# A mixer layer's output projection: residual and first y blocks loaded ahead, last row pair reordered

## The chip, the cores and the metric

One core of a Trainium2 chip runs the whole kernel. The metric is the device time of one execution in microseconds (us); before the change it is 945.74 us, the median of 3 runs (945.64 to 947.35). Engines are named as the profile names them: PE (TensorE; PEld its weight loads), DVE (VectorE), ACT (ScalarE), POOL (GpSimd) and SP (SyncE, which issues the DMAs here).

## The reference

One layer over 2048 tokens of width 1024, in float32. Branches A, B and C each make part of y; the change concerns the last line.

```python
h = jnp.einsum('bsd,de->bse', x, w_in)
a_u, a_v, a_g, b_val, b_glu, b_g, c_q, c_f, c_i, c_g = jnp.split(h, offsets, axis=-1)
y_a = _sgu_mixer(a_u, a_v, sgu_ln_g, sgu_ln_b, sgu_w, sgu_b) * jax.nn.silu(a_g)
y_b = _conv_module(b_val, b_glu, conv_w, conv_b, conv_ln_g, conv_ln_b) * jax.nn.silu(b_g)
y_c = _hgrn2_mixer(c_q, c_f, c_i, lb, hgrn_norm_g) * jax.nn.silu(c_g)
y = jnp.concatenate([y_a, y_b, y_c], axis=-1)
y = jnp.einsum('bse,ed->bsd', y, w_out)
return _layernorm(DEEPNORM_ALPHA * x + y, post_ln_g, post_ln_b)
```

## The kernel before, in words

The sequence is worked in two halves of two groups of 512 tokens. Each half runs branch B, then values, branch C and branch A in an order of its own (first half: B, A, values, C; second half: B, values, C, A), so that branch A of the second half stands right before the output projection. Every float32 matmul is made of three (`three`, L198): operands are split into a high and a low part (`split`, L144: a cast on ACT, a subtraction on DVE), and high x high, low x high and high x low are accumulated in one PSUM bank. Every branch stores its y, transposed, to `y_dr` in DRAM through SP (`y_store`, L229; the store at L230).

Branch A (`sgu`, L730) projects u and the gate for two feature tiles (ft) of two groups (gi); each ends with a mix matmul, `mx` (L632) and `ay` (L636) on DVE, and the store of ay. After a group, `free_c` (L782) is called: after group 0 it closes branch C's memory and loads blocks 0 to 2 of the transformed output weights (`wo_load`, L720, two DMAs of 1 MB a block, from `wo_dr`), and blocks 3 and 4 into the memory of that group's x; after group 1 blocks 5 and 6 into the memory of the last group's x.

The output projection takes 16 row blocks of 128 tokens as 8 pairs. A pair is a 2 x 2 block product in Strassen's manner (Winograd's form): seven products of 12 matmuls each (`product`, L842) of y blocks a11, a12, s2, s3, s1, a22, s4 with weight blocks wo[0], [1], [2], [3], [4], [6], [5]. `y_blocks` (L804) loads four raw pieces (ry) from y_dr, makes the sums (ysa, ysb; L833 to L837) and splits them into four tiles, a (a11, a12), s (s2, s3), t (s1, s4) and b (a22). The trace names the operands by these: `wh_y_a`, `wh_y_s`, `wh_y_t`, `wh_y_b`. Four of the products accumulate on one bank z (`poz`): a11, then s2, s1 and s4 on top of it, and between them DVE reads z out into the residual (`plus`, L884: alpha times x plus z); a12 goes into `poa`, s3 and a22 into `pod`, both added by `join` (L887). So a product onto z waits until the read-out ahead of it is done, and that read-out waits for the residual `xr`, which is loaded from x into one of four buffers (L879). `normed` (L849) then takes the layer norm of each row block: statistics on ACT (L859 to L862), for the very last row block on DVE (L854, L855); the reciprocal root on POOL (`rstd_of`, L223: an add and a power); two passes on DVE (L864, L867) and the store.

The order on each engine is not that of the program text: a scheduler orders the instructions at build time by a model of the chip's times, taking what is ready in the order of the text, and puts waits where data or memory require them. What stands late in the text can thus be executed early, if its memory is free. The order is fixed when the kernel runs; each engine and each DMA queue works through its own in order. A pool opened with `reuse_waits="tile"` waits for the release of each old tile that it covers, not of the whole pool.

Of the kernel before, what the change touches and what calls it, by code (L numbers as in the profile page):

```python
# [11 lines left out]
F32 = mybir.dt.float32  # L12
# [8 lines left out]
P = 128  # L21
# [62 lines left out]
def _body(tc, nc, d, ctx):  # L84
# [528 lines left out]
    def sgu_unit(g, gi, x, pl, vhat, w):  # L613
        if True:
            for ft in range(2):
# [15 lines left out]
                mx = pl.tile([P, 4, P], F32, tag="mx", bufs=2, name=f"mx{nm}")  # L631
# [98 lines left out]
    def sgu(hf, xs, pl, after):  # L730
# [3 lines left out]
        for gi in range(GPH):  # L734
            sgu_unit(hf * GPH + gi, gi, xs[gi], pl, vhat, w)
            after(gi)

    for hf in range(NHALF):
# [8 lines left out]
        if hf == 0:  # L747
            lower_bounds()
            sgu_setup()
            with ExitStack() as esw:  # L750
                wo_start(pool("wos", stack=esw, reuse_waits="tile"))
                with ExitStack() as esa:
                    pl = pool(f"a{hf}", stack=esa, reuse_waits="tile")
                    sgu(hf, xs, pl, lambda gi: None)
# [27 lines left out]
    def free_c(gi):  # L782
# [11 lines left out]
    with ExitStack() as esa:  # L794
        pl = pool("a1", stack=esa, side="right", reuse_waits="tile")
        sgu(NHALF - 1, xs, pl, free_c)


    NP = S // (2 * P)
    ot = pool("ot", stack=es, side="right", reuse_waits="tile")  # L800
    gb = ot.tile([P, 2, DM], F32, name="gb")
    nc.sync.dma_start(gb, d["post"])

    def y_blocks(p):  # L804
# [10 lines left out]
        out = {}  # L815
# [16 lines left out]
        pair("a", (a11, a12), ("a11", "a12"))  # L832
        nc.vector.tensor_add(s1, a21, a22)  # L833
        nc.vector.tensor_sub(s2, s1, a11)
        nc.vector.tensor_sub(s3, a11, a21)
        pair("s", (sa,), ("s2", "s3"))
        nc.vector.tensor_sub(s4, a12, s2)  # L837
        pair("t", (sb,), ("s1", "s4"))
        pair("b", (a22,), ("a22",))
        return out  # L840

    def product(out, y, blk, first):  # L842
        w = wo[blk].rearrange("p h (k n) -> p h k n", n=512)
        for kt in range(4):
            three(out, y[0][:, kt, :], y[1][:, kt, :], w[:, 0, kt, :], w[:, 1, kt, :],
                  first and kt == 0, kt == 3, skip_group_check=not first)
            tick(0.64)

    def normed(t, r, fine):  # L849
        mv = smp.tile([P, 2], F32, tag="omv", bufs=4, name=f"omv{t}")  # L850
        if fine:
            st = smp.tile([P, 2, 6], F32, name="ost")
            for n in range(2):
                nc.vector.bn_stats(st[:, n, :], r[:, n * 512 : (n + 1) * 512])  # L854
            nc.vector.bn_aggr(mv, st)  # L855
            rs = rstd_of(smp, mv[:, 1:2], 1, "ors")
        else:
# [101 lines left out]
```

## Time and profile before

| | before |
|---|---|
| median of 3 runs | 945.74 us (945.64 to 947.35) |
| the profiled execution: its time | 945.64 us |
| its span, first to last instruction | 943.9 us |
| PE busy | 912.6 us (97%) |
| PEld busy | 755.2 us (80%) |
| DVE busy | 710.6 us (75%) |
| ACT busy | 396.3 us (42%) |
| POOL busy | 81.7 us (9%) |
| mean granted TensorE clock | 0.989 |

Busy time is that of the span; matmuls overlap, so PE's busy share says only that matmuls follow one another. Times of the trace are counted from the span's start. The output projection is the stretch from 766.7 us to the end. The granted clock is a share of full speed: 1.0 is 2.4 GHz, 0.5 is 1.2 GHz. The shares of the whole span average over stages with different limits, so the rows below are all of single stretches.

### The profile page before, as it was taken

How to read it: one execution, taken by the hardware profiler on the slowest of the kernel's cores; microseconds unless marked ns; L12 is line 12 of the kernel's file. 1: busy time of each engine (PE TensorE's matmuls, PEld its weight loads, DVE VectorE, ACT ScalarE, POOL GpSimd, SP SyncE). 2: the span in 40 equal slices, each digit the busy share in tenths (PEclk: the TensorE clock that was granted, in tenths of full speed). 3: DMA queues.
4: the chain of work that ended last, by engine and by line, in shares of the span. 5: the costliest groups of instructions: out<-in, count | busy, mean ns of one | idle time of the engine just before them, and what ended most of it. 6: DMA issues, size and time to landing. Idle time of an engine off the chain costs nothing.

```text
span 943.9 us, 15786 instructions
## 1 busy us (share of the span) xinstructions
PE 912.6 (97%) x6045; PEld 755.2 (80%) x6045; DVE 710.6 (75%) x1605; ACT 396.3 (42%) x795; POOL 81.7 (9%) x129
## 2 busy tenths in 40 slices
PE   8999999999999999999999999999999996999994
PEld 6889888987777777788998777777798885888883
DVE  6998899736787669897997867778765235888885
ACT  6644363234354446542223435354544330634551
POOL 0001101000010000010000000000021000221121
PEclk9999999999999999999999999999999997999998
DMA  8756463111011104411111201111112987456422
GB/s 268 272 180 230 168 244 113 67 45 46 24 49 64 45 24 157 134 58 44 56 46 45 77 16 56 38 43 57 58 44 69 308 314 268 134 174 199 140 90 90
DMA packets 60812, 107.48 MB, mean 114 GB/s; under 512 B 5312, under 2 KB 21952, under 8 KB 60608
## 3 DMA queue, kind: packets, MB, share of 16 engines
q1 hardware_dynamic: 60736, 106.48, 33.0%
q8 instruction: 47, 0.77, 0.3%
q14 instruction: 29, 0.24, 0.1%
HBM read 75.00 MB, written 31.46 MB: 113 GB/s over the span
## 4 chain that ended last, share of the span: by engine, by line
PE 70%; DVE 16%; ACT 4%; DMA 3%; issue 3%; POOL 3%; SPq 0%; DVEq 0%; POOLq 0%; ACTq 0%
DVE acc L283 4%; PE poz L199 3%; PE pm_ci L200 3%; PE pm_ci L199 3%; PE pm_ci L201 3%; PE poz L200 3%; PE poz L201 3%; PE pm_q L199 3%; PE pm_q L201 3%; PE pm_q L200 3%; PE pm_f L199 2%; PE pm_f L200 2%; PE pm_f L201 2%; PE pm_cg L199 2%; PE pm_cg L201 2%
## 5 line engine op out<-in xcount | busy, mean ns | idle before, releaser
L283 DVE SCALAR_TENSOR_TENSOR acc<-bh,vec,acc 128x512 f32<-128x512 f32 x240 | 172.5, 746 | 2.2
L146 DVE TENSOR_TENSOR wl<-rw,wh 128x512 fp32r<-128x512 f32 x84 | 56.7, 686 | 29.2 <-ACT wh L145 29.2
L145 ACT CAST wh<-rw 128x512 fp32r<-128x512 f32 x84 | 50.1, 619 | 31.1 <-PE pm_f L200 11.1
L199 PE MATMUL pm_ci<-wh_ci,xhix 128*128 128x256 f32 x192 | 54.5, 284 | 0.0
L201 PE MATMUL pm_ci<-wh_ci,xlox 128*128 128x256 f32 x192 | 54.3, 283 | 0.0
L200 PE MATMUL pm_ci<-wl_ci,xhix 128*128 128x256 f32 x192 | 54.3, 283 | 0.0
L550 ACT ACTIVATE jk<-po 128x128 f32<-128x128 f32 x64 | 17.7, 277 | 60.7 <-PE po L545 59.8
L199 PE MATMUL pm_f<-xhix,wh 128*128 128x512 f32 x96 | 41.1, 429 | 0.0
L199 PE MATMUL pm_q<-xhix,wh 128*128 128x512 f32 x96 | 41.0, 427 | 0.0
L347 ACT COPY vh<-pm_ci 128x256 f32<-128x256 f32 x32 | 11.9, 373 | 65.7 <-PE pm_ci L201 65.6
L200 PE MATMUL pm_q<-xlox,wh 128*128 128x512 f32 x96 | 39.0, 407 | 0.0
L199 PE MATMUL pm_cg<-xhix,wh 128*128 128x512 f32 x96 | 39.0, 406 | 0.0
L201 PE MATMUL pm_q<-xhix,wl 128*128 128x512 f32 x96 | 37.8, 394 | 0.0
L201 PE MATMUL pm_f<-xhix,wl 128*128 128x512 f32 x96 | 37.8, 393 | 0.0
L200 PE MATMUL pm_f<-xlox,wh 128*128 128x512 f32 x96 | 37.6, 392 | 0.0
L201 PE MATMUL pm_cg<-xhix,wl 128*128 128x512 f32 x96 | 37.6, 391 | 0.0
L200 PE MATMUL pm_cg<-xlox,wh 128*128 128x512 f32 x96 | 37.5, 390 | 0.0
L199 PEld LDWEIGHTS pm_ci<-wh_ci,xhix 128*128 128x128 f32 x192 | 36.9, 192 | 0.0
L200 PEld LDWEIGHTS pm_ci<-wl_ci,xhix 128*128 128x128 f32 x192 | 36.9, 192 | 0.0
L201 PEld LDWEIGHTS pm_ci<-wh_ci,xlox 128*128 128x128 f32 x192 | 36.8, 192 | 0.0
L225 POOL TENSOR_SCALAR crs<-ss 128x4 f32<-128x4 f32 x16 | 3.6, 226 | 373.8 <-ACT jk L550 373.8
L884 DVE SCALAR_TENSOR_TENSOR xr<-xr,poz 128x512 f32<-128x512 f32 x32 | 21.7, 682 | 17.3 <-DMA xr<-x 13.2
(330 smaller groups left out, 2803.2 us busy)
## 6 DMA issues: line engine op xcount, KB each, us to landing
rw<-wf SPq DMA_DIRECT2D x84, 256.0 KB, 3.0
wob<-wo_dr SPq DMA_DIRECT2D x14, 1024.0 KB, 11.4
ry<-y_dr SPq DMA_DIRECT2D x32, 256.0 KB, 3.2
xr<-x SPq DMA_DIRECT2D x16, 512.0 KB, 4.4
out<-xr SPq DMA_DIRECT2D x15, 512.0 KB, 2.7
wo_dr<-wsh SPq DMA_DIRECT2D x28, 256.0 KB, 3.5
wo_dr<-wsl SPq DMA_DIRECT2D x28, 256.0 KB, 2.5
rx<-xT SPq DMA_DIRECT2D x24, 256.0 KB, 3.3
```

Of the source, the lines that this page charges most:

```text
L145: nc.scalar.copy(hi, src)
L146: nc.vector.tensor_sub(lo, src, hi.bitcast(F32))
L199: nc.tensor.matmul(out, wh, xh, start=first, stop=False, **kw)
L200: nc.tensor.matmul(out, wh, xl, start=False, stop=False, **kw)
L201: nc.tensor.matmul(out, wl, xh, start=False, stop=last, **kw)
L225: nc.gpsimd.tensor_scalar(r, mv_var, scale, EPS, ALU.mult, ALU.add)
L283: nc.vector.scalar_tensor_tensor(a, h[:, k : k + G], vcol(cw + k), a, ALU.mult, ALU.add)
L347: nc.scalar.copy(vh[:, gi * 4 + tt, vp * 256 : (vp + 1) * 256], pt[:, :256])
L550: nc.scalar.activation(jk, po[:, c * P : (c + 1) * P], AF.Square, accum_out=ss[:, c : c + 1])
L884: nc.vector.scalar_tensor_tensor(r[:, ns], r[:, ns], ALPHA, t, ALU.mult, ALU.add)
```

## The change

The residual `xr` gets a pool of its own, opened before branch A of the second half, and the loads for pairs 0 and 1 are issued there; later pairs are loaded two pairs ahead. `mx` and `ay` of branch A get one buffer instead of two. `y_blocks` becomes a generator, `y_steps`: its first two steps for pair 0 stand after ft 0 of group 1 in branch A, the rest after branch A; for later pairs the steps stand between the products of the pair before. The last pair gets an order of its own (a11, a12, s2, s4, s1, s3, a22): s4 goes to a bank of its own (z2), and a22 to another (d2), in two halves of 256 columns, each read out by itself. Both row blocks of the last pair take their statistics on DVE, piece by piece, and their reciprocal root as an add on DVE and a power on POOL. The diff, cut to its core:

```diff
-                mx = pl.tile([P, 4, P], F32, tag="mx", bufs=2, name=f"mx{nm}")
+                mx = pl.tile([P, 4, P], F32, tag="mx", bufs=1, name=f"mx{nm}")
...
-                y = pl.tile([P, G], F32, tag="ay", bufs=2, name=f"ay{nm}")
+                y = pl.tile([P, G], F32, tag="ay", bufs=1, name=f"ay{nm}")
...
+                after(gi, ft)
...
-    def free_c(gi):
+    def free_c(gi, ft):
+        if ft == 0:
+            if gi == 1:
+                first_y.append(y_steps(0))
+                for _ in range(2):
+                    next(first_y[0])
+            return
...
+    n0, n1 = slice(0, 512), slice(512, 1024)
+    ys, xr, first_y = {}, {}, []
+    xrp = pool("xr", stack=es, side="right", reuse_waits="tile")
+
+    def load_xr(p):
+        xr[p] = []
+        for k in range(2):
+            t = 2 * p + k
+            r = xrp.tile([P, DM], F32, tag="xr", bufs=4, name=f"xr{t}")
+            nc.sync.dma_start(r, d["x"][t * P : (t + 1) * P, :])
+            xr[p].append(r)
+
+    stiles = pool("stiles", stack=es, side="right")
+
+    def y_steps(p):
...
         pair("a", (a11, a12), ("a11", "a12"))
+        yield
         nc.vector.tensor_add(s1, a21, a22)
         nc.vector.tensor_sub(s2, s1, a11)
         nc.vector.tensor_sub(s3, a11, a21)
         pair("s", (sa,), ("s2", "s3"))
+        yield
         nc.vector.tensor_sub(s4, a12, s2)
         pair("t", (sb,), ("s1", "s4"))
+        yield
         pair("b", (a22,), ("a22",))
-        return out
-
-    def product(out, y, blk, first):
+
+    load_xr(0)
+    load_xr(1)
+    with ExitStack() as esa:
+        pl = pool("a1", stack=esa, side="right", reuse_waits="tile")
+        sgu(NHALF - 1, xs, pl, free_c)
+
+    for _ in first_y[0]:
+        pass
+
+
+    ot = pool("ot", stack=es, side="right", reuse_waits="tile")
+    gb = ot.tile([P, 2, DM], F32, name="gb")
+    nc.sync.dma_start(gb, d["post"])
+
+    def product(out, y, blk, first, cols=slice(0, 512)):
...
+    def store(t, r, rs, mv, parts):
         nc.vector.scalar_tensor_tensor(r, r, mv[:, 0:1], gb[:, 0, :], ALU.subtract, ALU.mult)
-        for n in range(2 if fine else 1):
-            ns = slice(n * 512, (n + 1) * 512) if fine else slice(0, DM)
+        for ns in parts:
             nc.vector.scalar_tensor_tensor(r[:, ns], r[:, ns], rs, gb[:, 1, ns], ALU.mult, ALU.add)
             nc.sync.dma_start(d["out"][t * P : (t + 1) * P, ns], r[:, ns])
 
...
+    def stats(t, r, parts):
+        st = smp.tile([P, len(parts), 6], F32, name=f"ost{t}")
+
+        def take(k):
+            nc.vector.bn_stats(st[:, k, :], r[:, parts[k]])
+
+        def done():
+            mv = smp.tile([P, 2], F32, tag="omv", bufs=4, name=f"omv{t}")
+            nc.vector.bn_aggr(mv, st)
+            rs = smp.tile([P, 1], F32, tag="orl", bufs=2, name=f"orl{t}")
+            nc.vector.tensor_scalar(rs, mv[:, 1:2], EPS, None, ALU.add)
+            nc.gpsimd.tensor_tensor(rs, rs, nhalf[:, :1], ALU.pow)
+            return rs, mv
+
+        return take, done
+
...
+        y = ys.pop(p)
+        r1, r2 = xr.pop(p)
+        ahead = y_steps(p + 1)
         z = bank("mm", 3, f"poz{p}")
         a = bank(("o", "st")[p % 2], 1, f"poa{p}")
         dd = bank("sc", 2, f"pod{p}")
-        product(z, y["a11"], 0, True)
-        plus(r1, n0, z)
-        product(a, y["a12"], 1, True)
-        product(z, y["s2"], 2, False)
-        plus(r2, n0, z)
-        join(r1, n0, a)
-        product(dd, y["s3"], 3, True)
-        product(z, y["s1"], 4, False)
-        plus(r2, n1, z)
-        join(r2, n1, dd)
-        product(dd, y["a22"], 6, False)
-        join(r2, n0, dd)
-        normed(2 * p + 1, r2, False)
-        product(z, y["s4"], 5, False)
-        plus(r1, n1, z)
-        normed(2 * p, r1, p == NP - 1)
+        if p < NP - 1:
+            product(z, y["a11"], 0, True)
+            plus(r1, n0, z)
+            product(a, y["a12"], 1, True)
+            next(ahead)
+            product(z, y["s2"], 2, False)
+            plus(r2, n0, z)
+            join(r1, n0, a)
+            product(dd, y["s3"], 3, True)
+            next(ahead)
+            product(z, y["s1"], 4, False)
+            plus(r2, n1, z)
+            join(r2, n1, dd)
+            product(dd, y["a22"], 6, False)
+            join(r2, n0, dd)
+            normed(2 * p + 1, r2)
+            product(z, y["s4"], 5, False)
+            for _ in ahead:
+                pass
+            plus(r1, n1, z)
+            normed(2 * p, r1)
+            if p + 2 < NP:
+                load_xr(p + 2)
+        else:
+            halves = (slice(0, 256), slice(256, 512))
+            take1, done1 = stats(2 * p, r1, (n0, n1))
+            take2, done2 = stats(2 * p + 1, r2, (n1,) + halves)
+            z2 = bank("mm", 3, f"poy{p}")
+            d2 = bank("sc", 2, f"poe{p}")
+            product(z, y["a11"], 0, True)
+            plus(r1, n0, z)
+            product(a, y["a12"], 1, True)
+            join(r1, n0, a)
+            take1(0)
+            product(z, y["s2"], 2, False)
+            plus(r2, n0, z)
+            product(z2, y["s4"], 5, True)
+            plus(r1, n1, z2)
+            product(z, y["s1"], 4, False)
+            join(r1, n1, z)
+            take1(1)
+            rs1, mv1 = done1()
+            plus(r2, n1, z)
+            product(dd, y["s3"], 3, True)
+            join(r2, n1, dd)
+            take2(0)
+            join(r2, n0, dd)
+            store(2 * p, r1, rs1, mv1, [slice(0, DM)])
+            for k, ns in enumerate(halves):
+                product(d2, y["a22"], 6, True, ns)
+                join(r2, ns, d2[:, ns])
+                take2(k + 1)
+            rs2, mv2 = done2()
+            store(2 * p + 1, r2, rs2, mv2, (n0, n1))
```

## Rows read from the trace of the kernel before

**Rows 1.** Stretches, projection's matmuls: bounds and length, PE and PEld busy (count), clock, DMA, GB/s.
```profile
766.60:780.60 14.00, 13.89 (x60) 11.19 (x60) 1.00 0.90 282
780.60:788.10 7.50, 0.00 (x0) 0.00 (x0) 0.66 1.03 417
788.10:793.40 5.30, 5.29 (x13) 4.18 (x14) 0.51 1.01 341
793.40:925.80 132.40, 132.13 (x577) 107.24 (x575) 1.00 0.43 144
```
**Rows 2.** Timeline of PE: start, duration, instruction, idle time before it and its releaser.
```profile
780.21 0.39 PE L201 MATMUL poa<-wob,wl_y_a 128*128 128x512 f32 x1
788.11 0.79 PE L199 MATMUL poz<-wob,wh_y_s 128*128 128x512 f32 x1 [7.51 <-DVE xr L884]
...
925.69 0.39 PE L201 MATMUL poz<-wob,wl_y_t 128*128 128x512 f32 x1
926.86 0.50 PE L199 MATMUL poz<-wob,wh_y_t 128*128 128x512 f32 x1 [0.78 <-DVE xr L884]
```
**Rows 3.** Chain that ended last, in order of time: start, length, what.
```profile
772.45 0.87 SPq L802
773.42 13.92 DMA xr<-x
```
**Rows 4.** Timeline of SP's DMA issues: start, length of merged issues, their count.
```profile
757.87 0.33 SPq L230 DMA_DIRECT2D y_dr<-ay  x1
765.78 0.52 SPq L724 DMA_DIRECT2D wob<-wo_dr  x1
769.57 0.33 SPq L230 DMA_DIRECT2D y_dr<-ay  x1
769.95 1.87 SPq L724 DMA_DIRECT2D wob<-wo_dr  x3
```
**Rows 5.** Timeline of DVE and POOL after the last matmul.
```profile
932.63 0.69 DVE L884 SCALAR_TENSOR_TENSOR xr<-xr,poz 128x512 f32<-128x512 f32 x1 [1.13 <-PE poz L201]
...
934.36 2.48 DVE L864 SCALAR_TENSOR_TENSOR xr<-xr,omv,gb 128x1024 f32<-128x1024 f32 x2
...
939.29 1.41 DVE L867 SCALAR_TENSOR_TENSOR xr<-xr,ors,gb 128x512 f32<-128x512 f32 x2 [0.72 <-POOL ors L226]
...
935.78 1.47 POOL L226 TENSOR_TENSOR ors<-ors,nhalf 128x1 f32<-128x1 f32 x1
...
938.70 0.55 POOL L226 TENSOR_TENSOR ors<-ors,nhalf 128x1 f32<-128x1 f32 x1
```
**Rows 6.** Timeline of ACT and DVE in branch A.
```profile
765.56 0.62 ACT L145 CAST wh_y_b<-ry 128x512 fp32r<-128x512 f32 x1 [2.48 <-PE pm_ag L200]
...
713.58 1.28 DVE L146 TENSOR_TENSOR wl<-rw,wh 128x512 fp32r<-128x512 f32 x2
```
**Rows 7.** Stretches: PE, PEld, DVE, ACT, POOL busy (count), clock, DMA share, GB/s.
```profile
671.00:684.00 13.00, 12.97 (x112) 10.49 (x112) 9.89 (x29) 6.50 (x21) 1.32 (x2) 1.00 0.17 62
...
828.00:847.00 19.00, 19.00 (x84) 15.45 (x83) 16.11 (x21) 8.53 (x15) 3.73 (x4) 1.00 0.49 166
```
**Rows 8.** Issues at 771.2 (wob) and 757.9 us (ay): size, us to landing.
```profile
wob<-wo_dr SPq DMA_DIRECT2D x1, 1024.0 KB, 12.4
...
y_dr<-ay SPq DMA_DIRECT2D x1, 256.0 KB, 11.1
```
**Rows 9.** DVE groups, 828 to 847 us: count | busy us, mean ns | idle before.
```profile
L146 DVE TENSOR_TENSOR wl_y_s<-ysa,wh_y_s 128x1024 fp32r<-128x1024 f32 x1 | 1.2, 1226 | 0.0
...
L834 DVE TENSOR_TENSOR ysa<-ysb,ry 128x512 f32<-128x512 f32 x1 | 0.7, 684 | 0.0
```
**Rows 10.** Timeline of PE and DVE in branch A: pieces of 256 columns.
```profile
690.02 0.28 PE L201 MATMUL pm_av<-wh_av,xlox 128*128 128x256 f32 x1
690.14 0.28 PE L199 MATMUL pm_av<-wh_av,xhix 128*128 128x256 f32 x1
...
714.86 0.43 DVE L607 BATCH_NORM_STATS2 ast<-vg 128x6 f32<-128x256 f32 x1
```

More of the change, by code (lines that the diff above doesn't have):

```diff
@@ L611, in sgu_values, with sgu_unit @@
         return vhat
-    def sgu_unit(g, gi, x, pl, vhat, w):
+    def sgu_unit(g, gi, x, pl, vhat, w, after):
         if True:
@@ L734, in sgu @@
         for gi in range(GPH):
-            sgu_unit(hf * GPH + gi, gi, xs[gi], pl, vhat, w)
-            after(gi)
+            sgu_unit(hf * GPH + gi, gi, xs[gi], pl, vhat, w, after)
     for hf in range(NHALF):
@@ L814, in y_blocks @@
         a11, a12, a21, a22 = raw
-        out = {}
+        out = ys[p] = {}
         def pair(nm, srcs, names):
@@ L843, in product @@
+    gb = ot.tile([P, 2, DM], F32, name="gb")
+    nc.sync.dma_start(gb, d["post"])
+    def product(out, y, blk, first, cols=slice(0, 512)):
         w = wo[blk].rearrange("p h (k n) -> p h k n", n=512)
         for kt in range(4):
-            three(out, y[0][:, kt, :], y[1][:, kt, :], w[:, 0, kt, :], w[:, 1, kt, :],
-                  first and kt == 0, kt == 3, skip_group_check=not first)
+            three(out[:, cols], y[0][:, kt, :], y[1][:, kt, :], w[:, 0, kt, cols],
+                  w[:, 1, kt, cols], first and kt == 0, kt == 3, skip_group_check=not first)
@@ L864, in normed @@
         nc.vector.scalar_tensor_tensor(r, r, mv[:, 0:1], gb[:, 0, :], ALU.subtract, ALU.mult)
[L865 to L866 removed]
+        for ns in parts:
             nc.vector.scalar_tensor_tensor(r[:, ns], r[:, ns], rs, gb[:, 1, ns], ALU.mult, ALU.add)
             nc.sync.dma_start(d["out"][t * P : (t + 1) * P, ns], r[:, ns])
+    def normed(t, r):
+        mv = smp.tile([P, 2], F32, tag="omv", bufs=4, name=f"omv{t}")
+        jk = ot.tile([P, DM], F32, tag="ojk", name=f"ojk{t}")
+        nc.scalar.activation(jk, r, AF.Identity, scale=1.0 / DM, accum_out=mv[:, 0:1])
+        nm = smp.tile([P, 1], F32, tag="onm", bufs=4, name=f"onm{t}")
+        nc.scalar.activation(nm, mv[:, 0:1], AF.Copy, scale=-1.0)
+        nc.scalar.activation(jk, r, AF.Square, bias=nm, accum_out=mv[:, 1:2])
+        store(t, r, rstd_of(smp, mv[:, 1:2], 1, "ors", 1.0 / DM), mv, [slice(0, DM)])
@@ L870, in _body, with plus, join @@
     smp = pool("smp", stack=es, side="right")
-    stiles = pool("stiles", stack=es, side="right")
-    n0, n1 = slice(0, 512), slice(512, 1024)
+    def plus(r, ns, t):
+        nc.vector.scalar_tensor_tensor(r[:, ns], r[:, ns], ALPHA, t, ALU.mult, ALU.add)
+    def join(r, ns, t):
+        nc.vector.tensor_add(r[:, ns], r[:, ns], t)
     for p in range(NP):
-        y = y_blocks(p)
-        xr = []
-        for k in range(2):
-            t = 2 * p + k
-            r = ot.tile([P, DM], F32, tag="xr", bufs=4, name=f"xr{t}")
-            nc.sync.dma_start(r, d["x"][t * P : (t + 1) * P, :])
-            xr.append(r)
-        r1, r2 = xr
-        def plus(r, ns, t):
-            nc.vector.scalar_tensor_tensor(r[:, ns], r[:, ns], ALPHA, t, ALU.mult, ALU.add)
-        def join(r, ns, t):
-            nc.vector.tensor_add(r[:, ns], r[:, ns], t)
+        y = ys.pop(p)
+        r1, r2 = xr.pop(p)
+        ahead = y_steps(p + 1)
```

25 lines of the change are left out of this document (2 added, 23 removed).

## The prediction, made before the change was run

> **What bounds the kernel now.** I read the stretches of the output projection first, then the matmuls around their gap, then the chain that ended last, the DMA issues, and last the tail. [rows 1]: the projection is bound by TensorE at the higher clock: 577 matmuls in 132.4 us, a pitch of 0.23 us. Three stretches are not. After five products (60 matmuls) no matmul runs for 7.5 us while the DMA share is 1.03, and then 13 matmuls take 5.3 us at a granted clock of 0.51 (the 1.2 GHz level). [rows 2]: the gap runs from 780.21 to 788.11 and its releaser is the first addition of the residual (L884), which reads xr. The matmul that waits, the s2 product of pair 0, accumulates on bank z, so z must be read out before it. [rows 3]: the chain of work goes from the issue of gb into one transfer of xr, 13.92 us from issue to landing. [rows 3, 4]: xr was issued at 773.42 behind three issues of wob and one of gb; the queue was full, not idle, as the DMA share of 1.03 in [rows 1] says. The third loss is in the last pair, [rows 2]: 0.78 us idle at 926.86, again a read-out of z. Last, TensorE ends at 932.63 where the final read-out begins, and the span ends at 943.9: a tail of 11.27 us [rows 5].
>
> Branch A, 714 to 766 us, is no target: the y blocks of pair 0 were already made there. The last of them, the cast for a22, runs at 765.56, before the projection's first matmul at 766.7 [rows 1, 6]. The scheduler had hoisted them although they stand behind branch A in the program. So of "prepared during branch A" only the residual is new.
>
> **The change, part by part.** All terms are against the profiled execution: 943.9 us of span and 945.64 of time, so 1.74 outside the span; that execution is 0.1 under the median of 945.74.
>
> *Residual loaded before branch A.* Four issues of 512 KB move past branch A's weight loads, its y stores and all fourteen wob issues on SP. Where they now stand the DMA share is 0.17 [rows 7], so 2 MB fit at the 417 GB/s of [rows 1] in 5 us. Behind them on SP stand weight loads whose buffers are split only from 713.58 [rows 6], some 30 us later; that cover hides them. What goes: the gap, 7.90 minus one pitch 0.23 = 7.67 us, and the slow stretch, 5.3 minus 13 x 0.23 = 2.3 us, since without idle time there is nothing after which the clock fell. Sum **-10.0**.
>
> *What is late next.* Without the wait on xr the products of pair 0 can follow one another: 12 x 0.23 = 2.73 us each, from 766.7. Their weights are the seven wob blocks. Block 6 is the last: its second half was issued at the end of the three merged issues (771.2) and took 12.4 us, landing at 783.6 [rows 4, 8]. Nothing in the change makes it earlier: its buffer is x of group 3, which branch A's last projection reads; block 5, held up in the same way, was first issued at 765.78 [rows 4]. With a11, a12, s2, s3, s1, s4 first, a22 wants it at 766.7 + 6 x 2.73 = 783.1: **+0.5 us**. In program order a22 comes before s4 and wants it at 780.4: +3.2 us, and perhaps the slow clock again (+2.3). Which it is depends on the scheduler's order, which the trace of before doesn't show; I take the first, because it did fill TensorE with products of pair 1 (five products before the gap, two of them of pair 1) rather than wait in program order. Ends for this term: 0 and +5.5.
>
> *mx and ay with one buffer.* mx is written and read on VectorE in order: nothing. ay now waits for the store of the ay before. The store issued at 757.87 took 11.1 us (769.0) [rows 4, 8], and the last ay was written 0.7 us before its store at 769.57, so from 768.85: a wait of 0.15 us. Behind it on VectorE stands the first read-out of z, which has a product (2.73 us) to spare; behind its store on SP stand three wob issues, so block 6 lands up to 0.15 later. Inside the 0.5 above.
>
> *y steps of the next pair between the products.* The same instructions as before in another program order; a pair takes VectorE 16.11 of 19 us, in which TensorE does the 84 matmuls of a pair without a gap [rows 7]. Before, they were hoisted likewise. I take 0; the bound above is the rival below.
>
> *Last pair.* s4 and a22 get banks of their own, so s4 no longer waits for z: 1.17 - 0.23 = **-0.9** (925.69 to 926.86 in [rows 2]). a22 in two halves is 24 matmuls of 256 columns at 0.12 (690.02 to 690.14, [rows 10]) instead of 12 at 0.23: **+0.1**.
>
> *Tail.* Before, behind 932.63: plus and stats of row block 14, two passes of 1.28 us of both row blocks, and a GpSimd queue in which row block 15's pow stands ahead of 14's (935.78 to 937.25), then 1.41 us of final passes from 939.29 and 3.2 us from their end (940.70) to 943.9 [rows 5]. After: let t0 be the end of s3. VectorE's pieces start about 0.6 us apart for 512 columns and 1.2 for 1024. From the end of s1 (t0 - 2.73) to the aggregate of the last row block it has join, stats, aggregate, eps, plus (0.6 + 0.6 + 0.2 + 0.2 + 0.6), the first pass of block 14 (1.2), join, stats, join (1.8), the second pass of 14 (1.2), then twice join and stats of 256 columns (0.35 + 0.4 each, from 0.43 us for a 256-column stats in [rows 10]), aggregate and eps (0.4): 8.1 us, to t0 + 5.4. TensorE ends at t0 + 24 x 0.12 = t0 + 2.9. So VectorE, not TensorE, sets this end, 2.5 us behind it; a first pass (1.2), two halves of the second (1.3), 0.3 for the pow, which at the 1.47 us of [rows 5] ends that much after the first pass, and 3.2 to the end of the span: 8.5 us of tail instead of 11.27, **-2.8**. Ends: 7.2 if the second pass of 14 is put behind the last aggregate, 10 if a pow is queued once more. The eps step on VectorE has no row; nearest are the aggregate (0.2) and GpSimd's step of the same size, which it replaces; I take 0.2.
>
> A rule bears on that pow. [rows 5]: it took 1.47 us beside two passes of VectorE with two SBUF inputs, 0.55 with VectorE idle. The Trainium skill (SBUF — State Buffer, Who interferes with whom) says that VectorE with two SBUF inputs and a GpSimd instruction that reads SBUF exclude one another, and the loser waits for the whole instruction. By that the pow, released as the first pass begins, costs up to 0.9 us more than 0.55; the sum with 0.55 would be 0.3 lower, and the rows side with the rule.
>
> Sum: -10.0 + 0.5 - 0.9 + 0.1 - 2.8 = **-13.1**: span 930.8, time **932.5**.
>
> **The rivals.**
> *Block 6 is asked for in program order* (a22 before s4). For: the program says so, and the order is fixed before the run, by times that needn't be the chip's; the wob transfers ran long (12.4 us for 1 MB). Against: the hoisting seen in before. Price: 3.2 + 2.3 instead of 0.5, so 937.5.
> *The change does not do what it says*: xr is placed late, or waits on SP for memory of branch B and still lands behind wob. For: the order on the queue is the scheduler's. Against: long before the wob loads the DMA share is 0.17 [rows 7], so there is room for even a late release. Then only the last pair gains: 945.64 - 0.9 + 0.1 - 2.8 = 942.0.
> *VectorE holds z in every pair* (the slower side). The s step of the next pair, three sums (0.68 us each, 0.6 apart) and a split of 1.2 us [rows 9], 3.0 us, now stands ahead of the read-out of s1's z, and the next z product (s4) has one product, 2.73 us, as cover. If the queue has it all there, after a read-out and a join (1.2), s4 waits some 1.5 to 2 us a pair, times seven: 10 to 14 us, and 932.5 becomes 943 to 946.5. It decides from 13.1 / 7 = 1.9 us a pair. For: VectorE has only 2.9 us idle in 19 [rows 7]. Against: the scheduler starts what is ready, and before, with the same work, TensorE waited under 0.5 us at a pair's boundary (132.4 us for 577 matmuls, [rows 1]). A milder form, 0.5 to 0.8 a pair, gives 936 to 938.
>
> **How the numbers follow.** The forecast 0.5 (930 to 934), block 6 in program order 0.27 (935 to 939), a mild VectorE loss 0.1 (936 to 939), xr still late 0.06 (942), z held in full 0.07 (943 to 947). Range 929.5 to 939.5: the low end is no wait for block 6 and the 7.2 us tail, less some of the 0.1 us waits at the pairs' boundaries; the high end takes in block 6's full price with a little of the VectorE loss, and leaves out 0.13. About 0.2% (1.9 us) is what a measurement of this kernel can tell from no change. Faster by more: 0.90; within: 0.05; slower: 0.05.
>
> **What would show each step.** xr issued before 700 us, with no matmul waiting for L884 between 775 and 795, shows the first term; a granted clock of 1.0 there shows the second. A wait of TensorE between 778 and 790 whose next matmul reads a wob block shows block 6; that it lies ahead of a22 tells which order it was. Row blocks ending with under 9 us behind the last matmul, and VectorE without idle time from s3 to the aggregate, show the tail. TensorE waiting for L884's successor once a pair, or a pair over 19.3 us, shows the slower rival. The prediction is wrong if branch A grows (matmuls waiting for weights near 714), or if block 6 lands well past 784.

## The result, and the profile after

The changed kernel takes 939.78 us (median; 937.91 to 940.73), the kernel before beside it 945.69 (945.12 to 947.35): that is 5.9 us faster by the medians. The measured ratio to the kernel before is 0.9926 with a 95% interval of 0.9911 to 0.9941. It isn't the quotient of these two medians, and it makes the gain 7.0 us (5.6 to 8.4). The forecast was 932.5, 13.1 faster. The measured median lies 0.3 us above the range's upper end (939.5); the ratio times the 945.74 of before gives 938.7, 0.8 us under it. The direction was right, the size was about half. The profiled execution has a span of 937.6 us and a time of 939.29.

In all fences "xr", "poz", "pod" and so on are the program's tile names. In the new source L910 is the first addition of the residual (L884 before), L913 the join, L877 and L879 the two passes of the layer norm, L895 its statistics on VectorE, L845 to L850 the sums of a y block, L821 the load of its raw pieces, L725 that of wob, L867 that of gb.

Stretches of the kernel after, where the projection starts at 766.95 (columns: length, busy time of PE, PEld, DVE, ACT, POOL with counts, granted clock, DMA share, GB/s):

```profile
766.00:786.00 20.00, 19.57 (x96) 15.69 (x97) 7.29 (x11) 3.45 (x5) 0.00 (x0) 1.00 0.89 285
786.00:806.00 20.00, 18.05 (x77) 13.90 (x76) 17.37 (x23) 9.58 (x16) 4.61 (x4) 1.00 0.60 189
...
920.00:938.00 18.00, 6.73 (x39) 5.69 (x37) 11.03 (x19) 0.00 (x0) 3.04 (x2) 0.76 0.23 88
```

The gap of 7.5 us and the stretch at the 1.2 GHz level of [rows 1] are gone: in the first 20 us TensorE is busy 19.57 us at full clock. TensorE now loses time in the second stretch (18.05 of 20) and in the last one. What it waits for, from 760 us on (us in total, times, longest):

```profile
PE poe L199 <- DVE xr L913: 3.2, 1, 3.2
PE poz L199 <- DVE xr L910: 1.6, 2, 1.2
PE pod L201 <- DVE wl_y_s L146: 0.5, 1, 0.5
PE pod L199 <- DMA wob<-wo_dr: 0.4, 1, 0.4
PE pod L199 <- ACT wh_y_s L145: 0.2, 1, 0.2
```

The same waits in the timeline of PE (start, duration, instruction, in brackets the idle time before it and its releaser):

```profile
785.52 0.50 PE L199 MATMUL pod<-wob,wh_y_b 128*128 128x512 f32 x1 [0.43 <-DMA wob<-wo_dr]
...
792.84 0.50 PE L199 MATMUL pod<-wob,wh_y_s 128*128 128x512 f32 x1 [0.18 <-ACT wh_y_s L145]
...
794.10 0.50 PE L201 MATMUL pod<-wob,wl_y_s 128*128 128x512 f32 x1 [0.53 <-DVE wl_y_s L146]
...
798.83 0.50 PE L199 MATMUL poz<-wob,wh_y_s 128*128 128x512 f32 x1 [1.24 <-DVE xr L910]
...
927.98 0.39 PE L199 MATMUL poe<-wob,wh_y_b 128*128 128x256 f32 x1 [3.22 <-DVE xr L913]
```

At 785.52 a22 of the first pair waited for wob block 6. From 792.84 to 798.83 the second pair waited three times around its s products: twice for the split of y_s, and once (1.24 us) for a read-out of z. At 927.98 the second half of the last a22 waited for the read-out of the first half. None of the last four was a term of the forecast.

Two timelines say why. SP's DMA issues (start, length of the merged issues, count), and VectorE at the start and at the end:

```profile
673.76 1.80 SPq L810 DMA_DIRECT2D xr<-x  x4
...
771.31 0.33 SPq L230 DMA_DIRECT2D y_dr<-ay  x1
771.69 1.89 SPq L725 DMA_DIRECT2D wob<-wo_dr  x3
773.68 1.28 SPq L867 DMA_DIRECT2D gb<-post  x1
775.00 18.01 SPq L821 DMA_DIRECT2D ry<-y_dr  x6
```
```profile
770.00 0.69 DVE L910 SCALAR_TENSOR_TENSOR xr<-xr,poz 128x512 f32<-128x512 f32 x1 [0.94 <-PE poz L201]
770.60 0.68 DVE L636 TENSOR_TENSOR ay<-mx,gu 128x512 f32<-128x512 f32 x1
...
788.77 0.68 DVE L845 TENSOR_TENSOR ysb<-ry,ry 128x512 f32<-128x512 f32 x1
...
924.53 1.28 DVE L913 TENSOR_TENSOR xr<-xr,pod 128x512 f32<-128x512 f32 x2
925.72 0.69 DVE L895 BATCH_NORM_STATS2 ost<-xr 128x6 f32<-128x512 f32 x1
926.33 1.27 DVE L879 SCALAR_TENSOR_TENSOR xr<-xr,orl,gb 128x1024 f32<-128x1024 f32 x1
927.51 0.41 DVE L913 TENSOR_TENSOR xr<-xr,poe 128x256 f32<-128x256 f32 x1
...
930.00 0.42 DVE L913 TENSOR_TENSOR xr<-xr,poe 128x256 f32<-128x256 f32 x1 [1.61 <-PE poe L201]
...
931.25 1.28 DVE L877 SCALAR_TENSOR_TENSOR xr<-xr,omv,gb 128x1024 f32<-128x1024 f32 x1
932.97 1.41 DVE L879 SCALAR_TENSOR_TENSOR xr<-xr,orl,gb 128x512 f32<-128x512 f32 x2 [0.44 <-POOL orl L902]
```

The residual is issued at 673.76, some 100 us earlier than in [rows 3]. The last ay store stands at 771.31, that is 4.36 us after the projection's first matmul where it was 2.86 us in [rows 4]. Behind it stand the three wob issues, gb, and the last of the second pair's four raw pieces (its first three landed by 724 us). In the tail, the join of the first half (927.51) stands behind 3 us of other work of VectorE, and the second half's matmuls behind that join.

To compare executions, whose projection starts anywhere from 766.2 to 770.4, I use two measures of one profiled execution each. The **loss** is the time between the starts of following matmuls of the projection beyond their pitch, 0.227 us for 512 columns and 0.12 for 256, added up over the first 40 us of the projection and over all from 120 us on. The **tail** runs from the last matmul's end to the span's end. (In [rows 5] the tail was counted from the final read-out, 0.03 us later.)

| kernel | ratio to before, 95% interval | loss, first 40 us | loss, from 120 us | tail |
|---|---|---|---|---|
| before | 1 | 10.3 | 1.5 | 11.3 |
| after | 0.9926 (0.9911–0.9941) | 3.8 | 3.9 | 7.6 |
| xr_early | 1.0019 (1.0005–1.0033) | 9.8 | 2.3 | 11.7 |
| xr_scratch | 0.9960 (0.9945–0.9975) | 7.8 | 2.0 | 11.7 |
| steps_end | 0.9954 (0.9937–0.9971) | 5.6 | 4.8 | 7.6 |
| ay_inplace | 0.9938 (0.9919–0.9957) | 3.2 | 4.1 | 7.6 |
| gb_late | 0.9903 (0.9888–0.9919) | 0.8 | 5.1 | 7.6 |
| wob_first | 0.9886 (0.9867–0.9904) | 0.3 | 4.1 | 7.6 |
| last_pair | 1.0005 (0.9990–1.0019) | 11.0 | 5.5 | 7.6 |
| last_whole | 0.9970 (0.9956–0.9984) | 10.4 | 1.1 | 9.3 |
| own_bank | 0.9918 (0.9902–0.9934) | 4.4 | 0.7 | 9.4 |
| whole_a22 | 0.9911 (0.9893–0.9928) | 3.5 | 0.5 | 9.6 |
| best | 0.9864 (0.9848–0.9880) | 0.3 | 0.5 | 9.5 |
| best_act | 0.9875 (0.9859–0.9891) | 0.3 | 0.3 | 9.5 |

### The profile page after: what moved, and what is told of

Same layout as the page of the kernel before. It is cut to its first block, busy times and chain, and to the rows that moved or that the text cites. A ratio compares the mean times of both kernels' runs of the same rounds, so it can differ in the third digit from the quotient of the medians.

```text
span 937.6 us, 15803 instructions
## 1 busy us (share of the span) xinstructions
PE 911.4 (97%) x6057; PEld 752.4 (80%) x6057; DVE 712.9 (76%) x1614; ACT 393.7 (42%) x790; POOL 76.6 (8%) x127
## 5 line engine op out<-in xcount | busy, mean ns | idle before, releaser
L438 DVE COPY_PREDICATED ST<-msk,sc 64x192 f32<-64x192 int32 (+2 forms) x96 | 28.8, 300 | 5.5 <-PE sc L432 3.2
```

Of the source, the lines that this page charges most:

```text
L438: nc.vector.copy_predicated(ST[rr, :, 64 * m + j0 * b : 64 * m + (j0 + nj) * b], msk[rr, mo : mo + mw].unsqueeze(1).to_broadcast([64, 4, mw]),
```

## The experiments

My theory after the result: the start's gain came, and about 4 us of it went back to loads that stand behind the last ay store on SP; the last pair's gain went back to a bank that both halves of a22 share. Rival for the start: the y steps between the products hold VectorE, and so z. Rival for the end: the chain of VectorE and GpSimd takes the same time in any order.

### The last pair: own_bank, whole_a22

own_bank gives the second half of a22 a bank of its own; whole_a22 computes a22 as one product of 512 columns, with one join and one statistics step.

```diff
# own_bank
-            d2 = bank("sc", 2, f"poe{p}")
+            d2 = (bank("sc", 2, f"poe{p}"), bank("o", 1, f"pof{p}"))
# whole_a22
-            take2, done2 = stats(2 * p + 1, r2, (n1,) + halves)
+            take2, done2 = stats(2 * p + 1, r2, (n1, n0))
-            for k, ns in enumerate(halves):
+            for k, ns in enumerate((n0,)):
```

> The changed kernel, with the second half of the last a22 product in a bank of its own (o). Theory 'bank': in the changed kernel the second half cannot start until the first half has been read out of the same bank (3.2 us idle before it); with two banks it follows at once, TensorE ends 3.3 us earlier (about 926.6), VectorE's 1.6 us idle time before the last join goes, and the span gets 1.6 us shorter (936.0). Rival 'VectorE sets the end anyway' (the working of the prediction): TensorE ends earlier, the span changes by less than 0.3 us.

> The changed kernel, with a22 of the last pair as one product of 512 columns, one join and one piece of statistics. Theory 'bank': no gap inside a22, TensorE ends at about 926, and VectorE has two short pieces less (join and stats, 0.4 us each), so the span is 2.1 us shorter (935.5), more than with two banks. Rival 'halves pay': reading out half while the other half is computed is worth its pieces, so the span is no shorter than with two banks (936.0).

Measured: 938.79 and 938.69 us. No matmul waits in the last pair of either. From a22's first matmul to the span's end it is 12.4 us in both, 14.4 in the kernel after. VectorE of own_bank behind the last read-out of z:

```profile
924.94 0.69 DVE L913 TENSOR_TENSOR xr<-xr,poz 128x512 f32<-128x512 f32 x1 [1.34 <-PE poz L201]
...
930.17 1.27 DVE L879 SCALAR_TENSOR_TENSOR xr<-xr,orl,gb 128x1024 f32<-128x1024 f32 x1
931.36 0.41 DVE L913 TENSOR_TENSOR xr<-xr,poe 128x256 f32<-128x256 f32 x1
931.69 0.41 DVE L913 TENSOR_TENSOR xr<-xr,pof 128x256 f32<-128x256 f32 x1
...
932.80 0.24 DVE L899 BATCH_NORM_AGGREGATE omv<-ost 128x2 f32<-128x18 f32 x1
```

VectorE has no idle time from 924.94 to the aggregate, and TensorE ended at 930.04, before VectorE joined either half. What follows: the wait at 927.98 belongs to the shared bank, and it is gone with a second bank or with one product. The halves as such bring nothing, since VectorE sets the end either way. By the medians the gain over the kernel after is 1 us and not to be told from none by the intervals, so these two runs show the cause in the trace, not its price in time; last_pair and last_whole below show that. The Trainium skill (Perfetto Trace Analysis, Matmuls) says that independent groups of matmuls should rotate through different PSUM banks, so that the read-out of one overlaps the next. The trace agrees: 3.2 us of wait with one bank, none with two.

### The start: ay_inplace, wob_first

ay_inplace writes ay over mx and gives mx two buffers again, so that the last ay need not wait for the store before it. wob_first calls the loads of blocks 5 and 6 inside the last unit of branch A, ahead of its mix products and its ay store, instead of behind them.

```diff
# ay_inplace
-                mx = pl.tile([P, 4, P], F32, tag="mx", bufs=1, name=f"mx{nm}")
+                mx = pl.tile([P, 4, P], F32, tag="mx", bufs=2, name=f"mx{nm}")
-                y = pl.tile([P, G], F32, tag="ay", bufs=1, name=f"ay{nm}")
-                nc.vector.tensor_mul(y, mx.rearrange("p c t -> p (c t)"), gu)
+                y = mx.rearrange("p c t -> p (c t)")
+                nc.vector.tensor_mul(y, y, gu)
# wob_first
+                after(gi, ft, True)
...
-    def free_c(gi, ft):
+    def free_c(gi, ft, early=False):
+        if early != (gi == 1 and ft == 1):
+            return
```

> The changed kernel, with ay written over mx, which gets its two buffers back (the same memory). The only difference in the order around it is that the last ay stands ahead of the first read-out of z on VectorE again. Theory 'ay's single buffer': the last ay store leaves SP 1.7 us earlier (769.6), block 6 lands at 783.7 instead of 785.5, so the 0.6 us wait before a22 goes and the waits of 2.8 us in pair 1 (792 to 799) shrink by about 1.7: together -1.5 to -2.3 us. Rival 'VectorE's order': the waits in pair 1 come from the queue on VectorE, not from arrivals: -0.6 us at most.

> The changed kernel, with the loads of blocks 5 and 6 issued before the last ay store, and the raw pieces of pair 1 before gb on SP. Theory 'arrival': block 6 lands by 781, the raw pieces by 784; the 3.4 us of waits in pairs 0 and 1 go, -3 us. Rival 'VectorE's order': the wait before a22 goes (0.6), the others stay.

Measured: 941.07 and 936.22 us. In ay_inplace the last ay store is back at 2.86 us behind the projection's start (769.43 from 766.57) and the wait for block 6 is gone, but the second pair's waits stayed (its last raw piece landed at 787.6, behind gb), and the time can't be told from that of the kernel after. SP's issues and all waits of PE from 760 us on, in wob_first:

```profile
765.25 2.85 SPq L726 DMA_DIRECT2D wob<-wo_dr  x4
770.55 0.33 SPq L230 DMA_DIRECT2D y_dr<-ay  x1
770.97 5.94 SPq L824 DMA_DIRECT2D ry<-y_dr  x3
777.01 0.65 SPq L870 DMA_DIRECT2D gb<-post  x1
```
```profile
PE poe L199 <- DVE xr L916: 3.2, 1, 3.2
PE poz L199 <- DVE xr L913: 0.4, 1, 0.4
```

Block 6 landed at 779.7. Three raw pieces now also stand ahead of gb; the first of them, the last one of the second pair, landed at 781.4. All waits of the start are gone: its loss is 0.3 us, 10.0 less than before, which is the forecast's first term. The edit moved two things at once, the wob blocks and, by the scheduler's choice, the raw pieces; gb_late (below) moves a raw piece alone.

### One part of the change alone: xr_early, last_pair

xr_early is the kernel before with only the load of the residual moved ahead of branch A. last_pair is the kernel before with only the new last pair.

```diff
# xr_early (kernel before)
+    xrp = pool("xr", stack=es, side="right", reuse_waits="tile")
...
+    load_xr(0)
+    load_xr(1)
     with ExitStack() as esa:
...
-            r = ot.tile([P, DM], F32, tag="xr", bufs=4, name=f"xr{t}")
-            nc.sync.dma_start(r, d["x"][t * P : (t + 1) * P, :])
+        if p > 1:
+            load_xr(p)
```

> The kernel before, with the residual of pairs 0 and 1 loaded from a pool of its own before branch A, and nothing else (mx and ay keep two buffers, y blocks and last pair as before). Theory 'arrival': the idle 7.7 us and the slow 2.5 us go, and block 6 and the raw pieces of pair 1, which come late in both kernels, take 3 to 4 us back: -6 to -7 us against before (about 939). Rival 'the residual alone was late' (the prediction): -9.7 us (about 936).

> The kernel before, with the last pair of the changed kernel and nothing else. Theory 'bank': the wait on z goes (-1.05), the second half of a22 waits 3.4 for its bank, the tail behind the last matmul is 3.6 shorter, and the halves cost 0.15: -1 us against before, from 177.2 us (first matmul of the projection to the end of the span) to about 176. Rival (the prediction): -3.6 us.

xr_early missed what I expected of it: 948.92 us, not faster than before (ratio 1.0019). Its wait for z is gone, and another one stands almost in the same place. PE and VectorE of xr_early, and then the stretch behind that wait:

```profile
781.41 0.80 PE L199 MATMUL poz<-wob,wh_y_s 128*128 128x512 f32 x1 [5.30 <-ACT wh_y_s L145]
...
778.27 0.69 DVE L844 TENSOR_TENSOR ysb<-ry,ry 128x512 f32<-128x512 f32 x1 [1.43 <-DMA y_dr<-ay]
```
```profile
781.40:787.60 6.20, 6.15 (x14) 4.36 (x15) 4.41 (x6) 2.48 (x4) 0.00 (x0) 0.50 1.01 398
```

The first pair's y sums, which before were made in branch A, now start at 778.27, released by the store of the last ay (issued at 772.88, landed at 778.24). The sums read only the raw pieces; what ties them to that store is memory. In the kernel before the pool "ot" held xr and lay ahead of the sums' pool; without xr in it the sums' scratch can come to lie over branch A's buffers, and must wait until ay is stored. TensorE stood 5.3 us and then ran 14 matmuls at a granted clock of 0.50. That reading is a guess without xr_scratch.

last_pair came out nearer to the bank theory than to its rival, but without the 1 us that the theory promised: 947.88 us, 1.0005 of before (0.9990 to 1.0019). Its wait at the second half, and the stretch of that half:

```profile
935.97 0.58 PE L199 MATMUL poe<-wob,wh_y_b 128*128 128x256 f32 x1 [3.00 <-DVE xr L909]
```
```profile
936.00:939.00 3.00, 2.90 (x12) 2.60 (x12) 0.44 (x2) 0.00 (x0) 0.00 (x0) 0.52 0.44 175
```

The bank wait gives back everything that the new order gains, together with the half behind it, which ran at the 1.2 GHz level: its 12 matmuls took 2.9 us, where 12 at 0.12 take 1.4. That was not in the theory.

### Settling both: xr_scratch, last_whole

xr_scratch is xr_early with the pool of the y sums reserved before branch A's pool, and one buffer each for mx and ay to make room for it; the y steps keep their old place at the start of a pair. last_whole is last_pair with a22 as one product.

```diff
# xr_scratch, against xr_early
-                mx = pl.tile([P, 4, P], F32, tag="mx", bufs=2, name=f"mx{nm}")
+                mx = pl.tile([P, 4, P], F32, tag="mx", bufs=1, name=f"mx{nm}")
-                y = pl.tile([P, G], F32, tag="ay", bufs=2, name=f"ay{nm}")
+                y = pl.tile([P, G], F32, tag="ay", bufs=1, name=f"ay{nm}")
...
     xrp = pool("xr", stack=es, side="right", reuse_waits="tile")
+    stiles = pool("stiles", stack=es, side="right")
...
     smp = pool("smp", stack=es, side="right")
-    stiles = pool("stiles", stack=es, side="right")
```

> The kernel before with the residual early (as in the run with that alone), and now also the pool of the y sums reserved before branch A's pool, with one buffer each for mx and ay so that it fits; the y steps keep their old place at the start of a pair, and the last pair is the old one. In the run with the early residual alone TensorE waited 5.5 us for the first pair's y_s, whose sums on VectorE started at 778.27, 0.03 us after the last ay store landed (778.24): there the sums' scratch lies over branch A's buffers. Scratch theory: with a place of its own the first pair's y steps run during branch A, neither the wait for y_s nor that for z is left at the first pair, and the slow stretch of the clock goes with them: -10.3 of the excess at the projection's start, +2 to +4 for block 6 and the second pair's raw pieces behind it, so 938 to 941 us, ratio 0.992 to 0.995, with tail and last pair as before. Order theory (the y steps' place between the products is what brings the gain, and the scratch has nothing to do with it): the wait at the first pair stays, 945 to 949 us.

> The kernel before with the new last pair alone (as in the run with that alone), but a22 as one product of 512 columns with one join and one statistics step. The new last pair in halves gave 1.0005 of before: there TensorE stood 3.05 us at the second half and ran that half at a lower clock. Bank theory: with the halves gone, the order and the separate bank for s4 are worth what they promised, -1 us of the wait for z and -1 to -2 us behind the last matmul: 943 to 945 us, ratio 0.997 to 0.998. Rival (the last pair's chain on VectorE and GpSimd costs the same in any order): 945.5 to 946.5 us, no difference to before.

xr_scratch: 942.77 us, 4 us faster than before, and about 6 faster than xr_early by the ratios. The first pair's y steps are back in branch A and neither z nor y_s of the first pair is waited for, as the scratch theory asked and the order theory excluded. (The single buffers for mx and ay, which make the room, came with it.) The time is above the 938 to 941 that I gave, because what is late next is dearer than I had put it. PE at the second pair, and the stretch behind:

```profile
797.11 0.50 PE L199 MATMUL pod<-wob,wh_y_s 128*128 128x512 f32 x1 [1.69 <-ACT wh_y_s L145]
...
799.46 0.80 PE L201 MATMUL pod<-wob,wl_y_s 128*128 128x512 f32 x1 [1.62 <-DVE wl_y_s L146]
```
```profile
797.00:804.50 7.50, 5.78 (x14) 4.29 (x15) 7.50 (x10) 2.66 (x5) 1.59 (x2) 0.58 0.70 238
```

There are two waits of 1.7 and 1.6 us, with two matmuls between, and the granted clock of the stretch is 0.58; in the kernel after the waits at this place are shorter (0.2, 0.5, 1.2) and the clock stays at 1.0.

last_whole: 944.30 us, 2.8 us faster than before. With one product the new order, the bank for s4 and the split of the statistics are worth that; in halves (last_pair) they are worth nothing that can be measured. The rival, that the end costs the same in any order, falls.

### The second pair: steps_end, gb_late

steps_end is the kernel after with the next pair's y steps all behind the pair's products. gb_late is the kernel after with gb issued behind the first y step of the second pair.

```diff
# steps_end
             product(a, y["a12"], 1, True)
-            next(ahead)
...
             product(dd, y["s3"], 3, True)
-            next(ahead)
...
             product(z, y["s4"], 5, False)
-            for _ in ahead:
-                pass
             plus(r1, n1, z)
             normed(2 * p, r1)
+            for _ in ahead:
+                pass
# gb_late
-    nc.sync.dma_start(gb, d["post"])
...
             next(ahead)
+            if p == 0:
+                nc.sync.dma_start(gb, d["post"])
```

> The changed kernel, with the y steps of the next pair all after the pair's products instead of between them; the first pair's steps stay in branch A and the last pair is the new one. Scratch theory: the place between the products is worth little, since VectorE has slack in a pair; within 1 us of the changed kernel, 938 to 941 us, with waits for y_s at the pairs' boundaries grown by at most some tenths of a us each. Order theory: y_s of each next pair comes late behind the layer norm's passes, 1 to 3 us in each of seven pairs: 945 to 955 us.

> The changed kernel; the load of gb (1 MB) is issued after the raw pieces of the second pair instead of before them. Blocks 5 and 6 stay behind the last ay store. In the changed kernel gb landed at 787.99 and the pieces at 788.6 to 790.1, and TensorE lost 2.8 us at the second pair. Queue theory (the pieces stand behind gb in SP's queue, and y_s of the second pair hangs on them): the pieces land 2 to 2.5 us earlier, the second pair's excess falls from 2.8 to under 1 us, block 6's wait of 0.6 stays: 937 to 938.5 us, ratio 0.990 to 0.991. If VectorE's own queue, and not the pieces, makes y_s late, the excess stays and the time is that of the changed kernel, 939 to 940.5 us.

steps_end: 942.90 us, above what the scratch theory gave and below what the order theory gave. From 40 us behind the projection's start on, it loses 6.3 us in all, the kernel after 6.1. The difference is at the second pair:

```profile
795.59 0.50 PE L199 MATMUL pod<-wob,wh_y_s 128*128 128x512 f32 x1 [1.71 <-ACT wh_y_s L145]
...
797.94 0.80 PE L201 MATMUL pod<-wob,wl_y_s 128*128 128x512 f32 x1 [1.62 <-DVE wl_y_s L146]
```

So the place between the products is worth some 2.5 us, once: where the last raw piece comes late, it puts more of the y steps ahead of the layer norm's passes of the first pair. Over 1 us of it is the clock, which was granted at 0.50 from 797.5 to 800.8. By the ratios the difference is 2.6 us, with intervals that just overlap.

gb_late: 938.24 us; the loss of the first 40 us falls from 3.8 to 0.8. Of these 3.0 us 0.6 is the wait for block 6, which I had expected to stay; block 6 landed 0.8 us earlier against the projection's start. SP's issues and the first y sum:

```profile
773.32 1.87 SPq L725 DMA_DIRECT2D wob<-wo_dr  x3
775.29 1.30 SPq L821 DMA_DIRECT2D ry<-y_dr  x1
776.69 0.74 SPq L927 DMA_DIRECT2D gb<-post  x1
777.48 1.55 SPq L821 DMA_DIRECT2D ry<-y_dr  x2
...
787.14 0.69 DVE L845 TENSOR_TENSOR ysb<-ry,ry 128x512 f32<-128x512 f32 x1 [3.22 <-DMA ry<-y_dr]
```

Only one raw piece moved ahead of gb, the last one of the second pair (the two others belong to the third). It landed at 787.04, 18.5 us behind the projection's start; in the kernel after it landed at 788.6, 21.7 us behind it. VectorE starts the sum 0.1 us after the landing in both (787.14 and 788.77). So one piece of 256 KB behind 1 MB on SP's queue made the second pair's sums 3.2 us late. The Trainium skill (DMA: Bandwidth & Descriptors, Queues, rings and completion order) says that an engine takes the descriptors of one ring in their order; the trace agrees in both kernels. gb itself landed at 790.8 and delayed nobody. The order changed as well, by the scheduler's choice: in the kernel after ScalarE works on the layer norm's statistics ahead of the cast of y_s, which starts 1.1 us after its sum is done (791.76), and in gb_late it casts y_s first (789.14). The cast comes 4.2 us earlier against the projection's start, the piece 3.2, so the arrival is the larger part and not all of it. In time the gain over the kernel after is 1.5 us by the medians, with intervals that overlap. In the trace 1.2 us went back from 120 us on, mostly because the second half of the last a22 now ran at a granted clock of 0.50.

### Both mended: best, best_act

best is wob_first with a22 as one product. best_act moves block 14's statistics from VectorE back to ScalarE.

```diff
# best_act, against best
-            take1, done1 = stats(2 * p, r1, (n0, n1))
...
-            rs1, mv1 = done1()
...
-            store(2 * p, r1, rs1, mv1, [slice(0, DM)])
+            normed(2 * p, r1)
```

> The changed kernel, with blocks 5 and 6 issued before the last ay store and a22 of the last pair in one product. If the two causes are separate they add up: 2.0 us from the tail, 3.4 us from the arrivals: from 170.6 us (first matmul of the projection to the end) to 165.2, span about 932, and faster than both kernels. If the tail's gain depended on the disturbed start, it would be the 167.2 of the run with the arrivals alone.

> As the run before it in this list, with the statistics of row block 14 on ScalarE, as in the other pairs, instead of VectorE. Theory 'VectorE sets the end of the tail': it loses two pieces of statistics, an aggregate and a small add (1.5 us) behind the last products, and the span gets up to 1 us shorter. Rival: GpSimd's two steps come late and the second pass of row block 14 delays the joins: no shorter.

best: 933.82 us, 0.9864 of before, and below the kernel after beyond both intervals. From 760 us to the last matmul TensorE waits once:

```profile
PE poz L199 <- DVE xr L913: 0.4, 1, 0.4
```

In its trace it is 165.2 us from the projection's first matmul to the span's end, where it was 177.2 in the kernel before. The expected figure was 165.2, so the two causes are separate and add up.

best_act: 934.42 us, no gain over best: VectorE then idles 1.44 us once, and the tail is the same 9.5 us.

## Why the prediction was right in sign and half in size

**Residual before branch A, -10.0: held.** No matmul waits for the first addition of the residual between 775 and 795, xr was issued at 673.76, and the clock of the first 20 us is 1.0, as the forecast asked. Branch A did not grow: from 720 to 765 us PE is busy 45.0 of 45 us in both kernels. wob_first, where nothing else is late, shows its size: loss 10.3 before, 0.3 there. But one reason in it was wrong in part. I said that of "prepared during branch A" only the residual is new, because the scheduler had already hoisted the first y blocks. It could do so only as long as their scratch was free; with the residual alone moved (xr_early) it was not, and nothing was gained. Reserving the sums' pool before branch A is a part of the change that I had not costed, and without it the first term did not come.

**What is late next, +0.5: this step failed on size.** It asked for the next load that the products wait for and stopped at block 6. Block 6 was asked for in the order that I took (s4's matmuls stand ahead of and between a22's) and cost 0.6 us, as forecast. The second pair then cost 2.8 us more, inside the ends that I had written for block 6 (0 to +5.5) but by another consumer: the last raw piece of its y stood behind block 6 and gb on the same queue. In [rows 3] gb and xr can be seen in that queue; the raw pieces behind them were not followed to their readers. gb_late and wob_first take the loss away. Half of it (the third wait, at 798.83) is a read-out of z that stands on VectorE behind the late y steps and a pass of the layer norm, so the slower rival's mechanism did come, once. I also wrote that block 6 could not come earlier, because of its buffer. That was wrong: in wob_first all four halves of blocks 5 and 6 were issued from 765.25 on, so it was the place behind the ay store on SP that held them.

**mx and ay with one buffer, inside the 0.5: too low.** I counted a wait of 0.15 us. The wait also changed the order on VectorE: the first read-out of z went ahead of the last ay, and the store behind which block 6 stands came 1.5 us later relative to the projection (770.00 and 770.60 in VectorE's timeline above). Block 6 landed at 785.5 instead of 783.6, past the 784 that I had named as a sign of being wrong. With ay written over mx (ay_inplace) that shift and the wait for block 6 are gone, but the time did not change beyond the intervals.

**y steps between the products, 0: not zero, but no loss.** steps_end puts it at 2.6 us in favour (0.9954 against 0.9926), by the traces at the second pair. From there on it is worth nothing, as costed. The slower rival, z held in every pair, did not show beyond the second pair.

**Last pair, -0.9 + 0.1: this step failed.** The wait of s4 for z is gone. But I let a22's halves follow one another at 0.12 us a matmul and did not ask which bank the second half writes: it is the first half's, which has to be read out by VectorE first, behind 3 us of its queue. That is the very queue that I had written down for the tail. The price was 3.2 us of wait in the kernel after; in last_pair it was 3.0 us and a second half at the 1.2 GHz level. In time it is 3.3 us, the difference between last_pair (1.0005) and last_whole (0.9970).

**Tail, -2.8: measured -3.7 in the kernel after, but that is not this step's number.** There the bank wait lets VectorE work off its queue before TensorE ends. Without that wait (own_bank) VectorE sets the end, as worked: the aggregate and the eps step end 6.0 us behind s3's last matmul, where I had 5.4. The tail is then 9.4 against the 8.5 forecast, so the step gives -1.9. The pieces that I listed from s1's end on add up to 8.3 us, not to the 8.1 that I wrote (so to t0 + 5.6 and a tail of 8.7), and own_bank took 8.3. The rest of the 0.6 is that two of s3's matmuls ran ahead of s1, so t0 comes 2.3 us behind s1's end instead of 2.7. The pow took 1.52 us beside a pass of VectorE, where I had taken 1.47. This agrees again with the rule of the Trainium skill (SBUF — State Buffer, Who interferes with whom) that it was weighed against; with VectorE idle it took 0.55 [rows 5].

Added up for the kernel after, by loss and tail: start -6.5, end +2.4, tail -3.7, and +0.8 between 40 and 120 us, which is spread over the pairs' boundaries and was not tried: -7.0. With the projection's start 0.2 later and 0.15 for the pitch of the halves that is -6.6, where the two spans differ by 6.3. With both new waits taken away (best) the ratio gives -12.9 (its interval: -11.3 to -14.4) and the traces -12.0, against the -13.1 of the sum. There the tail gives 1.0 less than forecast (9.5 instead of 8.5) and the 0.5 for block 6 is not paid. So the sum came near to what the change removes; it missed what the change adds. That the time came out at the upper end of the range was luck: I had put 935 to 939 down to block 6 in program order and to a VectorE loss in every pair, and neither is what happened.

**What stays open.** Why the projection starts at 766 in some profiled executions and at 769 or 770 in others was not studied; it is the work ahead of the change. That the scratch pool lies over ay in xr_early is read from the releaser of the first sum and from what xr_scratch mended, which also has one buffer for mx and ay; the addresses are not known. How much of the second pair's loss is the late piece and how much the scheduler's order is not separated by any run.

## What to carry to other kernels

When a wait goes, follow the queue behind it to each reader, not only to the next one: here the next load cost 0.6 us, and a piece of 256 KB behind it, with the order that followed from it, 2.8. Splitting a product to overlap its read-out needed a second bank here, and even with it brought nothing, because the engine that reads out was the one that set the end. A preparation that is "already early" in the trace may owe that to where its scratch lies, so a change that moves a pool has to be read as a change of order.

## What the runs showed of the hardware that I had not expected

TensorE's clock fell after waits that were short but close together: 1.7 and 1.6 us with two matmuls between them (xr_scratch) were followed by matmuls at a granted clock of 0.58 over 7.5 us; in the kernel after, waits of 0.2 and 0.5 us and then 1.2 us left it at 1.0. Behind the single wait at the second half of a22 it differed between kernels with the same idle time. The wait was 3.00 us in last_pair, and the clock then 0.52 over 3 us; it was 3.00 us in steps_end as well, and the clock stayed at 1.00. Behind a wait of 3.2 us the second half was granted 0.50 in gb_late, while in the kernel after 928 to 930 us were granted 0.80. The second half in steps_end, in gb_late and in the kernel after:

```profile
932.00:933.70 1.70, 1.62 (x12) 1.49 (x12) 0.45 (x2) 0.00 (x0) 0.00 (x0) 1.00 0.71 279
926.70:929.60 2.90, 2.86 (x12) 2.63 (x12) 0.43 (x1) 0.00 (x0) 0.00 (x0) 0.50 0.46 184
928.00:930.00 2.00, 1.96 (x12) 1.66 (x12) 0.39 (x2) 0.00 (x0) 0.00 (x0) 0.80 0.66 262
```

So a wait of TensorE in a forecast carries a slow stretch behind it as an upper end, and which of the two comes can't be read from the wait's length alone.
